# Gate and up projections begun over two of three tiles, the last tile's sums moved ahead of weight splits, and a second mixer's closing steps in another order

## The chip, the cores and the metric

The kernel runs on one core of a Trainium2 chip. A core has five engines with an instruction stream each: TensorE (PE, matrix products and transposes), VectorE (DVE), ScalarE (ACT), GpSimd (POOL) and SyncE (SP, which here only issues transfers). Each works through its stream in the order in which the build wrote it and waits on semaphores for the others. The metric is the time of one execution on the device in microseconds, the median over runs.

## The reference

A trunk of two layers over two groups of requests, 256 and 512 tokens of width 1024, all in fp32. Each layer is a token mixer (layer 0 windowed attention, layer 1 differential attention) and a SwiGLU channel mixer, both between RMS norms:

```python
def swiglu(h, w_gate_up, w_down):
    g, u = jnp.split(h @ w_gate_up, 2, axis=-1)
    return (jax.nn.silu(g) * u) @ w_down

def trunk(x, ...):
    for i in range(DEPTH):
        h = rms_norm(x, norm_mix_pre[i])
        ...
        x = x + rms_norm(m, norm_mix_post[i])
        h = rms_norm(x, norm_ffn_pre[i])
        x = x + rms_norm(swiglu(h, ffn_w_gate_up[i], ffn_w_down[i]), norm_ffn_post[i])
    return x
```

The hidden width D_FF is 2816. The mixer of layer 1 computes, for 8 heads, `(softmax(Q1 K1) - lambda softmax(Q2 K2)) V`, norms each head's result and multiplies by `w_o`.

## The kernel before

**Tiles and formats.** The 768 tokens are six tiles of 128. Activations that feed a product are kept transposed, three tiles side by side (384 columns, `HALF`): `h_hi[0]`, `h_lo[0]` hold tiles 0 to 2, `h_hi[1]`, `h_lo[1]` tiles 3 to 5. Each fp32 operand is split in two: `hi` is the rounded value (cast on ACT, L250 for weights, L331 for activations), `lo` the rest (a subtraction on DVE, L251 and L332). A product of two operands is three matmuls, hi·hi (L343), and the two mixed ones (L344, L345).

**Weights.** SP loads a raw block of 128x1024 (L224, tile `wraw` or `y_wraw`), ACT and DVE split it into `whi` and `wlo`. In gate and up the plain `wraw` tiles share two buffers; a load waits until the old block has been read for the last time. Split weights live in a ring of five units, and `free` starts the next split when a unit has been used. From the second pair on, units of gate and up come in twos from two raw blocks: four subtractions on DVE (L286 to L289) make combinations of the four quarter blocks, and the quarter called `b` is split as well.

**Gate and up (`ffn`).** They are computed by a scheme of the Strassen kind, which takes seven products for a two by two block product. The left operands are quarters of the activations and sums of them: a11, a12 (tiles 0 to 2, lower and upper half of the width), a22, s3, s1, s2, s4 (tiles 3 to 5). `combine` makes them, tile by tile in the order 0, 3, 1, 2, 4, 5: the transposes (L461), copies (L470, L475), sums (L477, L478, L479, L483) and splits (L331, L332). For each chunk c of the weights' columns the products accumulate in four banks of PSUM: X (`px`: p1 over a11, then p2 over a12), Y (`py`: p6 over s2, then p7 over s3), W (`pw`: p5 over s1, then p3 over s4) and Z (`pz`: p4 over a22). After p1 ACT copies X to `sv` (L1051), after p6 it copies Y to `u` (L1061), and only then may p7 add to the same bank; p2 ends with Silu (L1056). In chunk 0 and 1 p1 comes first, then p2 for both, then the same for chunks 2 and 3, and after that p4, p6, p5, p7 and p3 chunk by chunk. Each of these products is 12 matmuls (four slices of the contraction, three matmuls each).

**Around it.** The FFN begins while the mixer's last output tiles are still being finished: `later` holds the stages `c4, b5, d4, c5, d5` of the last two tiles (norm, scale, and as `d` the `combine`). A scheduler at build time orders each engine's instructions by their place in the program and by priority; parts under `tc.high_priority` go first, and `tc.issue_after` keeps one instruction behind another.

**End of the second mixer.** The steps of the last two heads are written out by hand in `run`: `S(h, t)` scores (`bsc`, L895), `T(h, t)` transposes of the weights of attention (`tpa`, L937), `V(h, t)` values (`pob`, L950, then L954, L956 on ACT and a scale on POOL, L963), `O(t, part)` transposes of the output heads (`tp_o`, L921). Between them stand pieces of the output product, `out[t]`: 24 matmuls of 512 columns in eight steps and an end, for the first half of the columns of tiles 0 to 2; `project` does the other tiles and the second half.

## Time and profile before

| | us |
|---|---|
| median of 3 runs | 1655.72 |
| the runs | 5599.19, 1655.11, 1655.72 |
| the profiled execution | 1656.38 |
| its span, first to last instruction | 1654.4 |
| PE busy | 1618.3 |
| DVE, ACT, POOL busy | 1222.8, 934.4, 170.7 |

The mean granted clock of PE in the profiled execution was 0.997. Layer 0's mixer ends and its gate and up products begin at about 291 us of the span, those of layer 1 at about 1157 us; the second mixer's closing steps lie around 1060 to 1107 us. The rows of the profile give a start in us, a duration in us, the engine, the line of the program, the operation, `out<-in` by the program's names, shapes, and in square brackets how long the engine had been idle and what released it. A time row of PE is longer than the distance to the next one, since matmuls are pipelined; what one costs is the distance of two starts.

### The profile page before, as it was taken

The numbers are of one execution on the slowest core, as the hardware profiler recorded it, in microseconds if no ns is written. First come the engines' busy times: TensorE is split into PE (matmuls) and PEld (weight loads), VectorE is DVE, ScalarE is ACT, GpSimd is POOL, SyncE is SP. The second block draws the span as 40 slices with busy tenths as digits, with TensorE's granted clock in tenths as the row PEclk, the third lists the DMA queues.
The fourth block names the chain that finished last, engine by engine and source line by source line (L and its number), as shares of the span: only waits on it lengthen the run. The fifth ranks groups of instructions, "written<-read, shape, count | busy, mean of one in ns | idle before, by whom it ended". The sixth has DMA issues, their size and how long they took to land. (4 is left out here: it accounts for less than half of the span.)

```text
span 1654.4 us, 24784 instructions
## 1 busy us (share of the span) xinstructions
PE 1618.3 (98%) x9163; PEld 1499.3 (91%) x9163; DVE 1222.8 (74%) x2167; ACT 934.4 (56%) x2038; POOL 170.7 (10%) x275
## 2 busy tenths in 40 slices
PE   7999999899999999999999999999899999999997
PEld 7888878899999998888999999888899999998886
DVE  7787756896766666888685886847896776656985
ACT  6777765654444444556475676766554444444553
POOL 1000001000000000001340461421000000000010
PEclk9999999999999999999999999999999999999999
DMA  6111104544333337675542332504443332337664
GB/s 217 40 39 49 37 16 153 178 137 139 101 131 110 131 116 246 239 253 180 156 111 69 98 84 79 152 1 166 153 156 123 117 125 97 131 129 254 228 238 159
DMA packets 70233, 220.64 MB, mean 133 GB/s; under 512 B 9249, under 2 KB 15521, under 8 KB 69857
## 3 DMA queue, kind: packets, MB, share of 16 engines
q1 hardware_dynamic: 54576, 175.93, 31.5%
q0 software_dynamic: 15392, 42.87, 9.1%
q8 instruction: 72, 1.18, 0.3%
q14 instruction: 49, 0.39, 0.1%
q10 hardware_dynamic: 144, 0.26, 0.0%
HBM read 163.59 MB, written 42.86 MB: 125 GB/s over the span
## 5 line engine op out<-in xcount | busy, mean ns | idle before, releaser
L251 DVE TENSOR_TENSOR wlo<-wraw,whi 128x1024 fp32r<-128x1024 f32 (+2 forms) x174 | 203.1, 1172 | 184.1 <-ACT whi L250 183.2
L250 ACT CAST whi<-wraw 128x1024 fp32r<-128x1024 f32 (+2 forms) x174 | 175.9, 1013 | 124.3 <-PE py L344 59.3
L343 PE MATMUL py<-hhi,whi 128*128 128x384 f32 x464 | 155.2, 335 | 0.3 <-ACT u L1061 0.3
L345 PE MATMUL py<-hhi,wlo 128*128 128x384 f32 x464 | 155.0, 334 | 0.0
L344 PE MATMUL py<-hlo,whi 128*128 128x384 f32 x464 | 155.0, 334 | 0.0
L331 ACT CAST hhi<-araw 128x768 fp32r<-128x768 f32 (+1 forms) x74 | 57.6, 782 | 91.3 <-DMA araw<-act 84.7
L343 PE MATMUL pv<-whi,hhi 128*128 128x512 f32 (+1 forms) x240 | 92.3, 385 | 0.0
L345 PE MATMUL pv<-whi,hlo 128*128 128x512 f32 (+1 forms) x240 | 92.2, 384 | 0.0
L344 PE MATMUL pv<-wlo,hhi 128*128 128x512 f32 (+1 forms) x240 | 92.1, 384 | 0.0
L332 DVE TENSOR_TENSOR hlo<-araw,hhi 128x768 fp32r<-128x768 f32 (+1 forms) x74 | 65.3, 889 | 32.6 <-ACT hhi L331 32.2
L343 PEld LDWEIGHTS py<-hhi,whi 128*128 128x128 f32 x464 | 87.1, 188 | 0.8 <-ACT u L1061 0.6
L344 PEld LDWEIGHTS py<-hlo,whi 128*128 128x128 f32 x464 | 87.1, 188 | 0.0
L345 PEld LDWEIGHTS py<-hhi,wlo 128*128 128x128 f32 x464 | 87.1, 188 | 0.0
L1114 POOL DMA_DIRECT2D act<-st x22 | 19.4, 882 | 636.6 <-DVE st L1113 636.6
L343 PE MATMUL po<-whi,hhi 128*128 128x512 f32 x192 | 78.4, 408 | 0.6 <-ACT hhi L331 0.6
L388 POOL TENSOR_TENSOR rstd_post<-rstd_post,mhalf 128x1 f32<-128x1 f32 x23 | 20.3, 885 | 544.9 <-ACT rstd_post L387 544.9
L345 PE MATMUL po<-whi,hlo 128*128 128x512 f32 x192 | 75.4, 393 | 0.9 <-DVE hlo L332 0.9
L901 ACT ACTIVATE be<-bsc,bmx 128x512 f32<-128x512 f32 (+1 forms) x96 | 58.7, 615 | 30.6 <-DVE bmx L899 30.0
L344 PE MATMUL po<-wlo,hhi 128*128 128x512 f32 x192 | 75.2, 392 | 0.0
L343 PE MATMUL px<-hhi,whi 128*128 128x384 f32 x208 | 69.8, 337 | 3.8 <-ACT hhi L331 2.8
L344 PE MATMUL px<-hlo,whi 128*128 128x384 f32 x208 | 69.7, 335 | 2.1 <-DVE hlo L332 2.1
L343 PE MATMUL pqa<-whi,hhi 128*128 128x384 f32 x192 | 71.1, 370 | 0.0
(307 smaller groups left out, 5049.0 us busy)
## 6 DMA issues: line engine op xcount, KB each, us to landing
act<-st POOLq DMA_DIRECT2D x22, 1344.0 KB, 6.6
wraw<-in_wgu SPq DMA_DIRECT2D x56, 512.0 KB, 4.7
araw<-act SPq DMA_DIRECT2D x70, 384.0 KB, 4.0
y_wraw<-in_wgu SPq DMA_DIRECT2D x40, 512.0 KB, 3.6
wraw<-in_wd SPq DMA_DIRECT2D x40, 512.0 KB, 4.0
xd<-x SPq DMA_DIRECT2D x18, 512.0 KB, 3.0
x<-xd SPq DMA_DIRECT2D x18, 512.0 KB, 4.3
wraw<-in_wo SPq DMA_DIRECT2D x16, 512.0 KB, 3.5
```

The costliest lines, as they stand in the source:

```text
L250: state["raw_hi"] = nc.scalar.copy(out=hi, in_=src)
L251: state["raw_lo"] = nc.vector.tensor_tensor(out=lo, in0=src, in1=hi.bitcast(F32), op=ALU.subtract)
L331: state["hi"] = nc.scalar.copy(out=hi, in_=src)
L332: state["lo"] = nc.vector.tensor_tensor(out=lo, in0=src, in1=hi.bitcast(F32), op=ALU.subtract)
L343: nc.tensor.matmul(out, ah, bh, start=start and i == 0, stop=False, skip_group_check=more)
L344: nc.tensor.matmul(out, ah, bl, start=False, stop=False, skip_group_check=more)
L345: nc.tensor.matmul(out, al, bh, start=False, stop=stop and i == last, skip_group_check=more)
L388: nc.gpsimd.tensor_tensor(out=r[:, :w], in0=r[:, :w], in1=mhalf[:, :w], op=ALU.pow)
L901: nc.scalar.activation(out=e[:, :n * P], in_=s, func=AF.Exp, bias=mx, accum_out=den[:, c:c + 1])
L1114: nc.gpsimd.dma_start(out=at_hand[c // 4][:, :, c // 2 % 2], in_=out.pop(c // 2))
```

## The change

Three things are changed. First, in `ffn` the first products of a layer (p1 of chunks 0 and 1; p4, p6 and p5 of chunk 0) are done by `early`: over the first two tiles' 256 columns for all the products of the group, and then over the third tile's 128 columns, kept behind. `mul` then skips them. All of p4(0), p6(0) and p5(0) so come before p7(0). Second, `combine` of tile 5 runs at high priority. Third, the hand-written list at the end of the second mixer weaves the output pieces of four tiles instead of three, in other places.

```diff
--- before.py
+++ after.py
@@ -340,7 +340,9 @@
 
         def step(i):
             (ah, al), (bh, bl) = pairs[i]
-            nc.tensor.matmul(out, ah, bh, start=start and i == 0, stop=False, skip_group_check=more)
+            m = nc.tensor.matmul(out, ah, bh, start=start and i == 0, stop=False, skip_group_check=more)
+            if i == 0:
+                state["first"] = m
             nc.tensor.matmul(out, ah, bl, start=False, stop=False, skip_group_check=more)
             nc.tensor.matmul(out, al, bh, start=False, stop=stop and i == last, skip_group_check=more)
 
@@ -509,7 +511,8 @@
 
         def stage_d():
             if comb is not None:
-                combine(y, t, f"h{sub + 1}_{t}", comb, o)
+                with tc.high_priority() if t == NT - 1 else ExitStack():
+                    combine(y, t, f"h{sub + 1}_{t}", comb, o)
                 return
             for s in transposes(y, t, f"h{sub + 1}_{t}"):
                 s()
@@ -1003,23 +1006,24 @@
             wk_o = column_blocks(take(4), 512)
 
             sq = {}
-            out = [out_unit(t, wk_o, o, 0, gp, sq, f"po1_0_{t}") for t in range(3)]
+            out = [out_unit(t, wk_o, o, 0, gp, sq, f"po1_0_{t}") for t in range(4)]
             S = lambda h, t: do(score, h * NT + t)
             T = lambda h, t: do(turn_e, h * NT + t)
             V = lambda h, t: do(values, h * NT + t)
             O = lambda t, part: turn_o[t][part:part + 1]
-            run = S(6, 3) + T(6, 1) + V(6, 0) + out[0][:2] + [lambda: turned(late)] + S(6, 4) + T(6, 2) + V(6, 1) + out[0][2:4]
-            run += S(6, 5) + T(6, 3) + V(6, 2) + out[1][:2] + S(7, 0) + T(6, 4) + V(6, 3) + O(0, 1) + out[1][2:4]
-            run += S(7, 1) + T(6, 5) + V(6, 4) + out[2][:2] + O(1, 1) + O(3, 0)
-            run += S(7, 2) + T(7, 0) + V(6, 5) + out[0][4:7] + O(2, 1)
-            run += S(7, 3) + T(7, 1) + V(7, 0) + out[1][4:7] + O(4, 0)
-            run += S(7, 4) + T(7, 2) + V(7, 1) + out[2][2:4] + O(0, 2) + O(5, 0)
-            run += S(7, 5) + T(7, 3) + V(7, 2) + out[0][7:] + O(1, 2) + O(3, 1)
-            run += T(7, 4) + V(7, 3) + out[2][4:7] + out[1][7:] + O(2, 2) + O(4, 1) + T(7, 5) + V(7, 4)
-            run += O(5, 1) + out[2][7:] + V(7, 5) + O(3, 2)
+            run = S(6, 3) + T(6, 1) + V(6, 0) + out[0][:3] + [lambda: turned(late)] + S(6, 4) + T(6, 2) + V(6, 1)
+            run += out[0][3:4] + out[1][:2] + S(6, 5) + T(6, 3) + V(6, 2) + out[1][2:4] + out[2][:1]
+            run += S(7, 0) + T(6, 4) + V(6, 3) + O(0, 1) + out[2][1:4]
+            run += S(7, 1) + T(6, 5) + V(6, 4) + O(3, 0) + O(1, 1) + out[0][4:7]
+            run += S(7, 2) + T(7, 0) + V(6, 5) + O(2, 1) + out[1][4:7]
+            run += S(7, 3) + T(7, 1) + V(7, 0) + O(4, 0) + out[2][4:7]
+            run += S(7, 4) + T(7, 2) + V(7, 1) + O(5, 0) + O(0, 2) + out[3][:3]
+            run += S(7, 5) + T(7, 3) + V(7, 2) + O(3, 1) + O(1, 2) + out[0][7:] + out[3][3:4]
+            run += T(7, 4) + V(7, 3) + O(4, 1) + O(2, 2) + out[1][7:] + out[3][4:7] + T(7, 5) + V(7, 4)
+            run += out[2][7:] + O(5, 1) + O(3, 2) + V(7, 5) + O(4, 2) + out[3][7:]
             for s in run:
                 s()
-        return project(o, 1, 2, lambda t: turn_o[t][2:], gp, g_next, wk_o, sq, 3)
+        return project(o, 1, 2, lambda t: turn_o[t][2:], gp, g_next, wk_o, sq, 4)
 
 
     def ffn(layer, later, comb, cpool, cstack, ostack, gains):
@@ -1030,11 +1034,29 @@
             "a11": (h_hi[0][:, 0:4], h_lo[0][:, 0:4]), "a12": (h_hi[0][:, 4:8], h_lo[0][:, 4:8]),
             "a22": (h_hi[1][:, 4:8], h_lo[1][:, 4:8]), "s3": (h_hi[1][:, 0:4], h_lo[1][:, 0:4]), **comb}
         steps = ExitStack()
+        begun, opened = set(), {}
+        two, third = slice(0, 2 * P), slice(2 * P, HALF)
         X, Y, Z, W, sv, ga, u2, u3, out = ({} for _ in range(9))
 
 
 
+        def early(banks, c, name, a, unit, part, cols):
+            if cols.start == 0:
+                banks[c] = bank(f"{name}{layer}_{c}")[:, :HALF]
+            ah, al = a_ops[a]
+            pairs = [
+                (tuple(v[:, part * 512 + k * P:part * 512 + (k + 1) * P] for v in unit), (ah[:, k, cols], al[:, k, cols]))
+                for k in range(4)]
+            if cols.start == 0:
+                products(banks[c][:, cols], pairs, True, True, True)
+                opened[c, name] = state["first"]
+            else:
+                with tc.issue_after(opened.pop((c, name)).ins):
+                    products(banks[c][:, cols], pairs, False, True, True)
+
         def mul(banks, c, name, a, unit, part, more=False):
+            if (c, name) in begun:
+                return
             if not more:
                 banks[c] = bank(f"{name}{layer}_{c}")[:, :HALF]
             ah, al = a_ops[a]
@@ -1157,7 +1179,12 @@
         c4, b5, d4, c5, d5 = later
         c4(), b5()
         u = take(2)
+        for cols in (two, third):
+            for c in range(2):
+                early(X, c, "px", "a11", u[c], 0, cols)
+        begun.update((c, "px") for c in range(2))
         p1(0, u[0]), p1(1, u[1])
+        begun.clear()
         d4()
         p2(0, u[0]), free(1), p2(1, u[1]), free(0)
         c5()
@@ -1176,9 +1203,16 @@
             return take(1)[0]
 
         u1, (u2_,) = take_u1(0), take(1)
+        for cols in (two, third):
+            early(Z, 0, "pz", "a22", u2_, 1, cols)
+            early(Y, 0, "py", "s2", u1, 1, cols)
+            early(W, 0, "pw", "s1", u2_, 0, cols)
+        begun.update(((0, "pz"), (0, "py"), (0, "pw")))
         p4(0, u2_)
         for c in range(AHEAD):
-            p6(c, u1), p5(c, u2_), p7(c, u1), c22(c), c21(c), free(0)
+            p6(c, u1), p5(c, u2_)
+            begun.clear()
+            p7(c, u1), c22(c), c21(c), free(0)
             if c + 1 < AHEAD:
                 u1, (u2_,) = take_u1(c + 1), take(1)
                 p4(c + 1, u2_)
```

The order of the instructions, before and after, at three places, the third of them on two engines. Names carry their numbers: `whi28` is weight unit 28, `wraw31` raw block 31, `py0_1` bank Y of layer 0, chunk 1, `oa5` a sum of tile 5.

PE at the start of layer 0's gate and up, around the first products of chunks 0 and 1. Before:

```order
L343 MATMUL px0_0_3749<-hhi0_110,whi24_3386 128x384
L343 MATMUL px0_1_3764<-hhi0_110,whi25_3658 128x384
L461 MATMUL tp_h1_4_1_3779<-ident_81,y_po0_1_4_3627 128x128 x4
L461 MATMUL tp_h1_4_0_3784<-ident_81,y_po0_1_4_3627 128x128 x4
L343 MATMUL px0_2_3852<-hhi0_110,whi26_3670 128x384
L344 MATMUL px0_0_3749<-hlo0_112,whi24_3386 128x384
```

After:

```order
L346 MATMUL px0_1_3762<-hlo0_112,whi25_3658 128x256
L347 MATMUL px0_1_3762<-hhi0_110,wlo25_3659 128x256
L343 MATMUL px0_0_3749<-hhi0_110,whi24_3386 128x128
L343 MATMUL px0_1_3762<-hhi0_110,whi25_3658 128x128
L463 MATMUL tp_h1_4_1_3803<-ident_81,y_po0_1_4_3627 128x128 x4
L346 MATMUL px0_0_3749<-hlo0_112,whi24_3386 128x128
```

Before, two products of 384 columns stand ahead of tile 4's transposes and of the first product with `hlo0`; after, 24 products of 256 columns do (the last two are the first rows here), and the transposes stand between products of 128 columns.

DVE between the `lo` splits of weight units 28 and 29. Before:

```order
L251 TENSOR_TENSOR wlo28_3703<-wraw29_3694,whi28_3702 128x1024
L332 TENSOR_TENSOR s1lo_0_3332<-oa4_233,s1hi_0_3331 128x4x128
L483 TENSOR_TENSOR oa1_230<-oa1_230,y_po0_1_4_3627 128x512
L251 TENSOR_TENSOR wlo29_3819<-wraw28_3674,whi29_3818 128x1024
L332 TENSOR_TENSOR s4lo_0_3336<-oa1_230,s4hi_0_3335 128x4x128
L332 TENSOR_TENSOR hlo1_113<-tp_h1_5_1_3882,hhi1_111 128x4x128
L477 TENSOR_TENSOR oa5_234<-tp_h1_5_0_3887,oa5_234 128x512
```

After (`wlo28` stands two rows above the first one, with tile 4's `s2lo` between):

```order
L332 TENSOR_TENSOR hlo1_113<-y_po0_1_4_3627,hhi1_111 128x4x128
L332 TENSOR_TENSOR s1lo_0_3332<-oa4_233,s1hi_0_3331 128x4x128
L479 TENSOR_TENSOR oa5_234<-tp_h1_5_0_3911,oa5_234 128x512
L332 TENSOR_TENSOR hlo1_113<-tp_h1_5_1_3906,hhi1_111 128x4x128
L480 TENSOR_TENSOR y_po0_1_5_3713<-tp_h1_5_0_3911,oa2_231 128x512
L481 TENSOR_TENSOR y_po0_1_5_3713<-oa5_234,oa2_231 128x512
L332 TENSOR_TENSOR s1lo_0_3332<-oa5_234,s1hi_0_3331 128x4x128
L332 TENSOR_TENSOR hlo1_113<-y_po0_1_5_3713,hhi1_111 128x4x128
L332 TENSOR_TENSOR s2lo_0_3334<-y_po0_1_5_3713,s2hi_0_3333 128x4x128
L485 TENSOR_TENSOR oa2_231<-oa2_231,y_po0_1_5_3713 128x512
L485 TENSOR_TENSOR oa1_230<-oa1_230,y_po0_1_4_3627 128x512
L251 TENSOR_TENSOR wlo29_3843<-wraw28_3674,whi29_3842 128x1024
```

Tile 5's sums and splits, which stood behind `wlo29`, now stand ahead of it, as does tile 4's `hlo`; `wlo29`, the last reader of `wraw28`, has 12 rows between it and `wlo28` where it had two.

PE at the first product of p7(0), `py0_0<-hhi1,whi28`. Before:

```order
L345 MATMUL py0_0_3975<-s2hi_0_3333,wlo28_3703 128x384
L345 MATMUL pw0_0_3991<-s1hi_0_3331,wlo29_3819 128x384
L343 MATMUL pz0_1_4044<-hhi1_111,whi31_3921 128x384
L344 MATMUL pz0_1_4044<-hlo1_113,whi31_3921 128x384
L343 MATMUL py0_1_4071<-s2hi_0_3333,whi30_3840 128x384
L344 MATMUL py0_1_4071<-s2lo_0_3334,whi30_3840 128x384
L345 MATMUL py0_1_4071<-s2hi_0_3333,wlo30_3841 128x384
L343 MATMUL py0_1_4071<-s2hi_0_3333,whi30_3840 128x384
L343 MATMUL py0_0_3975<-hhi1_111,whi28_3702 128x384
L344 MATMUL py0_0_3975<-hlo1_113,whi28_3702 128x384
```

After:

```order
L347 MATMUL pw0_0_4012<-s1hi_0_3331,wlo29_3843 128x128
L343 MATMUL pw0_0_4012<-s1hi_0_3331,whi29_3842 128x128
L346 MATMUL pw0_0_4012<-s1lo_0_3332,whi29_3842 128x128
L347 MATMUL pw0_0_4012<-s1hi_0_3331,wlo29_3843 128x128
L343 MATMUL py0_0_3999<-hhi1_111,whi28_3702 128x384
L346 MATMUL py0_0_3999<-hlo1_113,whi28_3702 128x384
```

Six products of chunk 1, which stood ahead of p7(0), now stand behind it, and the 128-column products of chunk 0 directly ahead of it.

ACT ahead of the copy of Y, `u20_0`, on which p7(0) waits. Before:

```order
L331 CAST s2hi_0_3333<-y_po0_1_5_3713 128x4x128
L250 CAST b2230_3842<-wraw31_3824 128x512
L250 CAST whi30_3840<-wraw31_3824 128x1024
L331 CAST s4hi_0_3335<-oa2_231 128x4x128
L250 CAST whi31_3921<-wraw30_3822 128x1024
L1061 COPY u20_0_3988<-py0_0_3975 128x384
```

After:

```order
L331 CAST s4hi_0_3335<-oa2_231 128x4x128
L1078 ACTIVATE ga0_3_3973<-px0_3_3891 128x384
L331 CAST s4hi_0_3335<-oa1_230 128x4x128
L250 CAST b2230_3866<-wraw31_3848 128x512
L250 CAST whi30_3864<-wraw31_3848 128x1024
L250 CAST whi31_3945<-wraw30_3846 128x1024
L1083 COPY u20_0_4061<-py0_0_3999 128x384
```

The casts of `wraw31` and `wraw30` (units 30 and 31) stand ahead of the copy in both; the cast `s4hi` of tile 2's sum moved from between them to ahead of them.

## Prediction

> **What bounds the kernel now.** I read the busy line first, then the waits of TensorE (PE), then the chain that ended last, then the timeline where the change moves rows.
>
> ```profile
> PE 1618.3 (98%) x9163; PEld 1499.3 (91%) x9163; DVE 1222.8 (74%) x2167; ACT 934.4 (56%) x2038; POOL 170.7 (10%) x275
> ```
>
> PE is busy 98% of a span of 1654.4 us, so a gain can only come out of its few gaps, and a loss is any new gap. The waits view lists the gaps by what ended them (total us, times, longest):
>
> ```profile
> PE py L344 <- DVE s2lo L332: 3.1, 2, 2.2
> PE px L343 <- ACT hhi L331: 2.8, 2, 1.5
> PE tpa L937 <- DVE be L909: 2.7, 1, 2.7
> PE px L344 <- DVE hlo L332: 2.1, 2, 1.1
> ...
> PE px L343 <- ACT sv L1051: 1.0, 1, 1.0
> PE po L345 <- DVE hlo L332: 0.9, 2, 0.7
> PE pz L343 <- ACT whi L250: 0.8, 1, 0.8
> PE tp_h L461 <- DVE y_po L397: 0.6, 2, 0.3
> ```
>
> All but the `tpa` row (second mixer) and the `po` row (not touched) stand at the heads of the two FFN layers, where the change works: 3.1 + 2.8 + 2.1 + 1.0 + 0.8 + 0.6 = 10.4 us, and 2.7 in the mixer. More than 13.1 us cannot be won by removing these. That is under 2% (33 us, about what a measurement of this kernel can tell from no change).
>
> Behind the `py <- s2lo` wait stands a loop that the chain of layer 1 shows (start, us, what):
>
> ```profile
> 1176.22 1.15 DVE wlo L251
> 1177.39 5.75 DMA wraw<-in_wgu
> 1183.39 0.63 ACT b L250
> ...
> 1190.78 0.35 PE py L343 x2
> ```
>
> A gate/up weight load takes one of two raw buffers and can start only when VectorE (DVE) has read the old contents for the last time, in the split `wlo`. Here the load is issued as `wlo` ends, and everything of the next weight unit follows its landing. The position of `wlo` on DVE sets it. Layer 0 has the same loop; the rows of DVE, of SP's queue, of ScalarE (ACT) and of PE:
>
> ```profile
> 309.11 1.22 DVE L251 TENSOR_TENSOR wlo<-wraw,whi 128x1024 fp32r<-128x1024 f32 x1
> 310.25 0.68 DVE L332 TENSOR_TENSOR s1lo<-oa,s1hi 128x512 fp32r<-128x512 f32 x1
> 310.85 0.68 DVE L483 TENSOR_TENSOR oa<-oa,y_po 128x512 f32<-128x512 f32 x1
> 311.45 1.22 DVE L251 TENSOR_TENSOR wlo<-wraw,whi 128x1024 fp32r<-128x1024 f32 x1
> ...
> 317.33 0.69 DVE L286 TENSOR_TENSOR wraw<-wraw,wraw 128x512 f32<-128x512 f32 x1 [0.46 <-DMA wraw<-in_wgu]
> ```
> ```profile
> 312.69 0.33 SPq L224 DMA_DIRECT2D wraw<-in_wgu  x1
> ```
> ```profile
> 320.50 1.06 ACT L250 CAST whi<-wraw 128x1024 fp32r<-128x1024 f32 x1 [2.56 <-DVE wraw L288]
> 321.46 0.61 ACT L331 CAST s4hi<-oa 128x512 fp32r<-128x512 f32 x1
> 321.97 1.04 ACT L250 CAST whi<-wraw 128x1024 fp32r<-128x1024 f32 x1
> 322.92 0.47 ACT L1061 COPY u<-py 128x384 f32<-128x384 f32 x1
> ...
> 333.48 0.48 ACT L1061 COPY u<-py 128x384 f32<-128x384 f32 x1 [1.71 <-DVE st L1103]
> ```
> ```profile
> 324.22 0.33 PE L343 MATMUL py<-hhi,whi 128*128 128x384 f32 x1
> 324.39 0.33 PE L344 MATMUL py<-hlo,whi 128*128 128x384 f32 x1
> ...
> 334.01 0.44 PE L343 MATMUL py<-hhi,whi 128*128 128x384 f32 x1 [0.27 <-ACT u L1061]
> ```
>
> The reader is to see: `wlo` of unit 29 (311.45) ends at 312.67 and the load of `wraw31` goes out at 312.69. DVE has it at 317.33, 4.6 us later. ACT then casts units 30 and 31 (320.50, 321.97) and only behind them copies `u` out of Y's bank (322.92). That copy lets p7(0), which accumulates s3 into the same bank, start (324.22).
>
> **The change, part by part.**
>
> *Split products.* Per layer 60 matmuls of 384 columns become 60 of 256 and 60 of 128. Start to start, 384 columns take 0.17 us (the rows at 324.22 and 324.39); narrower ones:
>
> ```profile
> 1629.83 0.28 PE L343 MATMUL pv<-whi,hhi 128*128 128x256 f32 x1
> 1629.95 0.28 PE L344 MATMUL pv<-wlo,hhi 128*128 128x256 f32 x1
> ```
> ```profile
> 25.07 0.51 PE L639 MATMUL tqa<-ident_r,sp 128*128 128x128 f32 x4
> 25.07 0.34 PE L639 MATMUL tqa<-ident_r,sp 128*128 128x128 f32 x2
> ```
>
> 256 columns take 0.12 us. The same four transposes shown whole and cut after two differ by 0.17, so 0.085 for 128. No row has a product of 128 columns in this format; the transposes are the nearest. A pair costs 0.12 + 0.085 − 0.17 = 0.035 us, 120 pairs 4.2 us. Ends: nothing (128 columns as a third of 384, 0.057; less is excluded, since the columns stay the same), or as dear as 256 columns, 0.12, 8.4 us. I take 4.2, but it need not reach the end: it lies ahead of the waits below, and PE would reach them early.
>
> The Trainium skill ("TensorE: Matmul & The Clock Gate", LDWEIGHTS) gives a weight load of P columns P/1.2 ns, 107 ns for 128. Were that the floor, a pair would cost 0.057 and all 6.8 us. The row's 0.085 is under it and is used.
>
> *The first px products.* In layer 0:
>
> ```profile
> 296.28 0.44 PE L344 MATMUL px<-hlo,whi 128*128 128x384 f32 x1 [1.07 <-DVE hlo L332]
> ```
>
> PE waited for tile 2's lo half. Now 24 products over tiles 0 and 1 (24 × 0.12 = 2.9 us) run where PE had waited for ACT's `hhi` (at most 1.5 us) and for this `hlo` (1.1). But `hlo` of tile 2 keeps its place on DVE, so PE waits again, until about 296.3. It then has 22 products of 128 columns (1.9 us) and four transposes left where it had 22 of 384 (3.8 us). That lead of about 1.5 us isn't kept: the next products accumulate into the banks that ACT copies into `sv`, and ACT now does those copies behind tile 4's copy, square and cast. I set the two against each other as 0 (ends: −3, when all px and tp_h waits of a layer go, and +1.5). Either end is swallowed by the wait at p7(0), below.
>
> *The last tile's sums first.* This carries the forecast. Between the splits of units 28 and 29 DVE now has 12 instructions where the rows above show 2; two of them stood ahead of unit 28's split before. So unit 29's split comes 8 × 0.60 (the distance of the rows at 310.25 and 310.85) = 4.8 us later. I add 0.6, one cast like 321.46's, for casts of tile 5 that DVE must await: 311.45 + 5.4 = 316.85. SP issues `wraw31` at 312.69 + 5.4 = 318.1. (The new order also puts the load of `y_wraw37` ahead of it on SP; that one waits for the sum into oa2, which DVE does before this split, so it adds nothing.) It lands by 317.33 + 5.4 = 322.7. From there the old rows took 320.50 − 317.33 = 3.2 us to unit 30's cast with five DVE instructions, now four: 2.6, so 325.3. Unit 31's cast follows without `s4hi` between them, 326.3; then the copy `u` 327.25, ended 327.7; p7(0) at about 327.8.
>
> PE is not late itself: its 36 + 36 split products of Z, Y and W take 36 × (0.12 + 0.085) = 7.4 us. They begin near 316.6 (an estimate: 24 px products, 4.1 us, behind the `sv` copies of chunks 2 and 3, which ACT now does behind tile 5's copy and cast, near 312.5) and end near 324. It waits some 3.9 us for a copy whose input is ready. Before, c = 1's first six products (1.0 us) were done by then; now none. Lateness at p7(0): 327.8 − 324.2 + 1.0 = 4.6. At p7(1), where PE waited 0.27 before, the copy `u` of 333.48 came after DVE's `st`, the end of a chain that starts from the next weights. Their buffers come free with the splits of units 30 and 31, which are late by what the landing is late, less one instruction of 0.6: 5.4 − 0.6 = 4.8 and a little for queueing. I take 5.2 us for the layer, between 4.6 and 5.4 + 0.6, and nothing given back, since behind that PE runs back to back again.
>
> What would take this away is ACT doing the copy ahead of the casts. The Trainium skill ("TensorE: Matmul & The Clock Gate", Architectural detail) says ACT and DVE are strict FIFO; the trace agrees: the copy starts at 322.92, right behind the cast that started at 321.97. Passing would leave only the wait for unit 30's weights, about 1 us per layer.
>
> Layer 1: the load issued at 1177.39 needs 5.75 us, so the same shift gives 1182.8 + 5.75 = 1188.55, unit 30's cast at 1191.2, the copy at 1193.1, p7(0) at 1193.7 against 1190.78: 2.9 + 1.0 = 3.9, and at p7(1) again about the shift of the loop, 5.0.
>
> *Second mixer's end.* Seven matmuls of 512 columns more stand ahead of the `tpa` transposes that waited 2.7 us. At 0.17 × 512 / 384 = 0.23 us each (an estimate from the rows of 384), 1.6 us of that wait go. In return the last `tp_o` transpose loses cover: 24 products (5.5 us) stood between it and the one before, now three (0.7). What feeds it ends on POOL:
>
> ```profile
> 1103.91 0.40 POOL L963 TENSOR_TENSOR ob<-ob,rstd_sub 128x128 f32<-128x128 f32 x1
> 1105.36 0.55 POOL L388 TENSOR_TENSOR rstd_sub<-rstd_sub,mhalf 128x1 f32<-128x1 f32 x1 [1.05 <-ACT rstd_sub L387]
> 1105.98 0.40 POOL L963 TENSOR_TENSOR ob<-ob,rstd_sub 128x128 f32<-128x128 f32 x1
> ```
>
> The last two tiles' `ob` come 2.1 us apart, so 2.1 − 0.7 = 1.4 us of a new wait show. Net −0.2; ends −2.7 (the old wait gone, no new one) and +2.5 (the old one stays in part and a second `tp_o` waits as long). I take 0.
>
> **Sum.** The profiled execution took 1656.4 us (span 1654.4), 0.7 above the median 1655.7. 1656.4 + 5.2 + 5.0 + 0 = 1666.6; against the median 1665.9. I say 1666.5.
>
> **Rivals.**
>
> *R1, the other side: the waits simply go.* DVE takes the last tile's sums in time it has to spare, and the copy `u` is there when PE comes. PE comes to p7(0) 3.9 us ahead of the forecast's copy, so it decides from there: unit 29's split by 316.85 − 3.9 = 312.95 and `wraw31` in by 318.8. Then 13.1 us of waits go and 4.2 come: 1656.4 − 13.1 + 4.2 = 1647.5. For it: DVE is 74% busy. Against: those ten rows follow each other without a gap, and the load is issued 0.02 us behind the split. Chance 0.11. By the price of a load in the Trainium skill, above, R1 would end at 1650.
>
> *R2, the loss grows.* The weight loop stays full in chunks 2 and 3, each adding a wait of about 1 us per layer as at `pz <- whi` (0.8): 1656.4 + 10.2 + 4 = 1670.6. For it: two raw buffers only. Chance 0.12.
>
> *R3, milder.* The load needs less than 4.6 us since it meets fewer others, or DVE is ahead by the 1 to 2 us it idles; about 2.5 us less per layer: 1661.5. Chance 0.15.
>
> **How the numbers follow.** Forecast 0.62 for 1663 to 1669, R1 0.11, R2 0.12, R3 0.15. The range 1657 to 1672 takes in R2, R3 and the mixer's ends and leaves out R1 and the far tails. No case reaches 33 us: faster 0.01, same 0.97, slower 0.02.
>
> **What the profile after would show.** A wait of `py` L343 (the first s3 product) for ACT's `u` of 3 to 5 us in each layer; `wlo` of unit 29 4 to 6 us after where it was against unit 28's; the `s2lo` and `whi` waits gone; `px <- hlo` still there; the 128-column products near 0.085 us apart. No wait at the `u` copies would make the forecast wrong and R1 right.

## The result and the profile after

| | median us | runs | profiled execution, its span |
|---|---|---|---|
| before | 1655.82 | 6 | 1656.38, 1654.4 |
| changed | 1669.74 | 6 | 1671.42, 1669.7 |

The ratio of changed to before is 1.0072, with a 95% interval of 1.0061 to 1.0083: slower by 0.72% of 1656 us, 12 us (the medians differ by 13.9). Two runs of the kernel before, one of 5599 us here and one of 2689 us beside the last experiment, are far off and enter no ratio. A second set of the changed kernel, below, gave 1.0079 (1.0065 to 1.0092). The forecast was 1666.5, in a range of 1657 to 1672.

Where the time went is read from the starts of the same instruction in both traces. The last addition to x of layer 0's mixer (L500, now L502) starts at 296.14 before and 298.07 after: 1.9 us late, in code that wasn't changed. The last gating product of layer 0's gate and up (L1103, now L1125) starts 7.3 us late, that is 5.4 more. The last addition to x of the second mixer is 8.4 late, 1.1 more. The last gating product of layer 1 is 15.3 late, 6.9 more, and so is the end of the span. The change costs 5.4 + 6.9 us in the two FFNs; the 1.9 and most of the 1.1 are scatter, which other executions below show as −0.3 to 1.7 and −1.6 to 3.1.

The busy line of the changed kernel's page, and its waits of PE (us in total, times, longest; without the 8.4 us at the kernel's entry):

```profile
PE 1631.4 (98%) x9283; PEld 1512.7 (91%) x9283; DVE 1224.8 (73%) x2167; ACT 934.5 (56%) x2038; POOL 169.3 (10%) x275
```
```profile
PE py L343 <- ACT u L1083: 5.9, 2, 3.0
PE px L343 <- ACT sv L1073: 3.9, 4, 2.3
PE px L346 <- DVE hlo L332: 2.5, 2, 1.4
PE tp_o L924 <- POOL ob L966: 2.3, 2, 1.5
...
PE tpa L940 <- ACT ob L957: 0.8, 1, 0.8
```

The wait of p7(0) for the copy `u` is new, 5.9 us in two pieces, one in each layer. The waits for `s2lo`, for `hhi` and for `whi` at `pz` are gone, those for `sv` and `hlo` are longer, and the mixer has exchanged 2.7 us of `tpa` for 1.0 more of `tp_o` and a `tpa` wait of 0.8. PE is busy 13 us longer although its share is the same: that is the 120 dearer pairs and, as will be seen, stretches at half clock.

The chain that ended last, in layer 1 (start, us, what):

```profile
1182.84 0.99 DVE wlo L251
1183.89 0.68 DVE s2lo L332
...
1189.98 1.20 DVE ob L485 x2
1191.19 1.15 DVE wlo L251
1192.35 4.85 DMA wraw<-in_wgu
1197.38 0.63 ACT b L250
...
1201.04 1.04 ACT whi L250
1202.08 0.38 ACT u L1083
1202.51 0.69 PE py L343
```

The chain now runs on DVE itself from one `wlo` (1182.84) through tile 5's sums and splits without a gap to the next `wlo` (1191.19), then through the load, the combinations, the cast and the copy `u` to PE. Before, the two `wlo` were 2.3 us apart (1173.81 and 1176.15 in the old trace). In layer 0 it is the same; rows of DVE, SP, ACT and PE:

```profile
309.08 1.22 DVE L251 TENSOR_TENSOR wlo<-wraw,whi 128x1024 fp32r<-128x1024 f32 x1
...
317.43 1.22 DVE L251 TENSOR_TENSOR wlo<-wraw,whi 128x1024 fp32r<-128x1024 f32 x1
```
```profile
318.67 11.40 SPq L224 DMA_DIRECT2D wraw<-in_wgu  x3
```
```profile
326.28 1.99 ACT L250 CAST whi<-wraw 128x1024 fp32r<-128x1024 f32 x2 [2.08 <-DVE wraw L288]
328.18 0.47 ACT L1083 COPY u<-py 128x384 f32<-128x384 f32 x1
```
```profile
328.70 0.69 PE L343 MATMUL py<-hhi,whi 128*128 128x384 f32 x1 [2.90 <-ACT u L1083]
```

`wlo` of unit 29 starts 317.43 − 309.08 = 8.4 us behind that of unit 28, where it was 2.3. The load of `wraw31`, the first of the three in SP's row, goes out behind it at 318.67; the casts of units 30 and 31 follow at 326.28, the copy `u` at 328.18, and p7(0) has waited 2.9 us.

What the prediction hadn't looked at stands in a table by stretches: us, then PE, its weight loads, DVE, ACT and POOL busy, and behind POOL's, ahead of the DMA share, the granted clock, the share of its full clock that TensorE was given. The changed kernel, from p7(0) of each layer on:

```profile
328.70:335.00 6.30, 6.30 (x20) 6.30 (x21) 4.34 (x7) 0.81 (x2) 0.00 (x0) 0.51 0.52 166
335.00:341.00 6.00, 6.00 (x37) 6.00 (x36) 4.09 (x9) 1.83 (x4) 0.00 (x0) 1.00 0.01 3
...
1202.50:1208.70 6.20, 6.19 (x19) 6.19 (x20) 4.10 (x7) 0.82 (x2) 0.00 (x0) 0.50 0.54 169
```

And the kernel before, behind its wait of 2.2 us for `s2lo` in layer 1:

```profile
1186.00:1189.90 3.90, 3.90 (x13) 3.90 (x14) 3.90 (x6) 2.88 (x4) 0.00 (x0) 0.56 0.41 126
```

Behind the wait PE runs at half clock for some 6 us: the matmuls of p7(0) start 0.32 us apart and not 0.173. In each layer 18 of them do, 2.6 us more. From 335 on the clock is full again, as the second row shows. In the FFNs of the kernel before it happened once (0.50 from 1186.5 to 1189.9), to 12 matmuls, 1.7 us. The changed kernel has one more such stretch, from 300.7 to 304.1 in layer 0; PE waits 0.2 us and 2.9 us behind it, so it is not read as a loss here.

### The profile page after: what moved, and what is told of

Same layout as the page of the kernel before. It is cut to its first block, busy times and chain, and to the rows that moved or that the text cites. A ratio compares the mean times of both kernels' runs of the same rounds, so it can differ in the third digit from the quotient of the medians.

```text
span 1669.7 us, 25027 instructions
## 1 busy us (share of the span) xinstructions
PE 1631.4 (98%) x9283; PEld 1512.7 (91%) x9283; DVE 1224.8 (73%) x2167; ACT 934.5 (56%) x2038; POOL 169.3 (10%) x275
## 5 line engine op out<-in xcount | busy, mean ns | idle before, releaser
L343 PE MATMUL px<-hhi,whi 128*128 128x384 f32 (+2 forms) x224 | 73.7, 330 | 3.9 <-ACT sv L1073 3.9
L346 PE MATMUL px<-hlo,whi 128*128 128x384 f32 (+2 forms) x224 | 73.6, 329 | 2.5 <-DVE hlo L332 2.5
L347 PE MATMUL px<-hhi,wlo 128*128 128x384 f32 (+2 forms) x224 | 73.3, 328 | 0.0
```

The source lines that it names most:

```text
L343: m = nc.tensor.matmul(out, ah, bh, start=start and i == 0, stop=False, skip_group_check=more)
L346: nc.tensor.matmul(out, ah, bl, start=False, stop=False, skip_group_check=more)
L347: nc.tensor.matmul(out, al, bh, start=False, stop=stop and i == last, skip_group_check=more)
```

## The experiments

For each run the loss in a layer is read as above: how late the last gating product of gate and up is, less how late the last addition to x of the mixer ahead of it is, both against the trace of before.

| run | median us | ratio to before, 95% interval | layer 0 | layer 1 |
|---|---|---|---|---|
| changed | 1669.74 | 1.0072 (1.0061 to 1.0083) | +5.4 | +6.9 |
| changed, again | 1671.44 | 1.0079 (1.0065 to 1.0092) | +4.2 | +7.3 |
| without the priority | 1661.50 | 1.0026 (1.0015 to 1.0037) | +1.9 | +2.0 |
| priority alone | 1655.40 | 0.9991 (0.9982 to 0.9999) | +0.5 | −2.1 |
| mixer's end alone | 1656.60 | 0.9999 (0.9991 to 1.0008) | −0.8 | −0.1 |
| changed, copy first | 1663.62 | 1.0046 (1.0032 to 1.0060) | +3.3 | +3.2 |
| changed, unit 29's split early | 1661.99 | 1.0032 (1.0020 to 1.0044) | +1.7 | +1.8 |
| Z, Y, W split alone | 1663.08 | 1.0034 (1.0021 to 1.0047) | +3.0 | +2.9 |
| X split alone | 1657.18 | 1.0003 (0.9995 to 1.0012) | +0.4 | 0.0 |
| before, copy first | 1651.44 | 0.9969 (0.9956 to 0.9981) | −4.3 | −2.0 |
| changed, both repairs | 1662.43 | 1.0032 (1.0020 to 1.0043) | +1.7 | +1.8 |
| changed, PE kept busy | 1671.07 | 1.0093 (1.0075 to 1.0111) | +5.8 | +9.0 |

The before's median beside these runs was 1656.2 to 1657.1.

**Without the priority.** The second part undone.

```diff
-                with tc.high_priority() if t == NT - 1 else ExitStack():
+                with ExitStack():
                     combine(y, t, f"h{sub + 1}_{t}", comb, o)
```

> The changed kernel with its second part undone: tile 5's sums at ordinary priority. The split wlo of unit 29 then stands 4 rows behind that of unit 28 on VectorE instead of 12 behind, 8 x 0.60 = 4.8 us earlier; the split products stay. Theory (late split, late load of raw block 31, ScalarE's casts of units 30 and 31, and the copy u behind them in order): p7(0)'s wait for u, 3.0 us in each layer, shrinks to under 1 us; what is left is TensorE's dearer products, 60 pairs x 0.058 us (0.120 + 0.111 - 0.173, from the changed kernel's rows) = 3.5 us a layer less the waits that they cover. 1659 to 1663. Rival 1 (the loss is the split products' own time on TensorE and their order ahead of p7): nothing comes back, 1668 to 1671. Rival 2 (the priority alone is the loss): 1654 to 1657.

Measured: 1661.5, as the theory has it. The new wait for `u` falls from 5.9 us in all to 2.5, and smaller ones come, `sv` 1.7 and `wlo` at `pz` 1.6 among them (its first rows behind the entry's: us in total, times, longest):

```profile
PE px L346 <- DVE hlo L332: 2.7, 2, 1.4
PE py L343 <- ACT u L1083: 2.5, 3, 1.7
```

At p7(0) only 0.2 of the 2.5 us are left, in layer 1. The others, 0.6 us in layer 0 and 1.7 in layer 1, are at p7(1), the same product of chunk 1. Two thirds of the loss come with the priority. The rest is there without it.

**The priority alone.** Only that line added to the kernel before.

```diff
-                combine(y, t, f"h{sub + 1}_{t}", comb, o)
+                with tc.high_priority() if t == NT - 1 else ExitStack():
+                    combine(y, t, f"h{sub + 1}_{t}", comb, o)
```

> The kernel before with the second part alone: tile 5's sums at high priority, no split products, the mixer as before. On VectorE the split of unit 29 is as late as in the changed kernel (11 rows between it and that of unit 28), but on ScalarE the copy u of bank Y now stands ahead of the casts of units 30 and 31. Theory (the late load hurts because the copy u stands behind the late casts): p7(0) doesn't wait for u; TensorE waits only for unit 30's weights after p7(0), about as long as it waited for them and for s2lo before: 1655 to 1659. Rival (a split that is late by 5 us costs 5 us a layer wherever the copy stands): 1664 to 1667.

Measured: 1655.4, no loss at all. This is the sharpest of the runs, since the split is as late as in the changed kernel. DVE's two `wlo` are 7.8 us apart, and unit 30 is cast at 326.19; but ACT's copy `u` (318.40) stands far ahead of the casts:

```profile
309.55 1.22 DVE L251 TENSOR_TENSOR wlo<-wraw,whi 128x1024 fp32r<-128x1024 f32 x1
...
317.30 1.22 DVE L251 TENSOR_TENSOR wlo<-wraw,whi 128x1024 fp32r<-128x1024 f32 x1
```
```profile
318.40 0.48 ACT L1062 COPY u<-py 128x384 f32<-128x384 f32 x1 [0.96 <-PE py L345]
...
326.19 2.11 ACT L250 CAST whi<-wraw 128x1024 fp32r<-128x1024 f32 x2 [1.26 <-DVE wraw L288]
```
```profile
328.36 0.44 PE L343 MATMUL pz<-hhi,whi 128*128 128x384 f32 x1 [1.86 <-ACT whi L250]
```

p7(0) runs while the load is under way, and PE waits only 1.9 us in layer 0, for the weights of chunk 1. That is no loss on balance, since the `s2lo` waits (3.1 us in the two layers) are gone too; waits for `whi` of 3.6 us, where there were 0.8, stand in their place. A late split alone doesn't cost 5 us; a late split with `u` behind its casts, and nothing else for PE to do, does. So 13.9 us isn't the sum of the parts: the priority alone gives −1.4, the rest without the priority +4.7, and together they lose 12 to 14.

**The mixer's end alone.** The third part on the kernel before.

```diff
-            out = [out_unit(t, wk_o, o, 0, gp, sq, f"po1_0_{t}") for t in range(3)]
+            out = [out_unit(t, wk_o, o, 0, gp, sq, f"po1_0_{t}") for t in range(4)]
...
-            run += O(5, 1) + out[2][7:] + V(7, 5) + O(3, 2)
+            run += out[2][7:] + O(5, 1) + O(3, 2) + V(7, 5) + O(4, 2) + out[3][7:]
...
-        return project(o, 1, 2, lambda t: turn_o[t][2:], gp, g_next, wk_o, sq, 3)
+        return project(o, 1, 2, lambda t: turn_o[t][2:], gp, g_next, wk_o, sq, 4)
```

> The kernel before with the third part alone, the other order of steps at the second mixer's end. Forecast: 0 (ends -2.7 and +2.5): the tpa wait of 2.7 us shrinks to about 1 and a tp_o wait of 1.4 us comes. 1655 to 1657. Rival (the new tp_o waits, 1.5 and 0.7 us in the changed kernel, outweigh it): 1658 to 1659.

Measured: 1656.6, the same within 0.1%. The old `tpa` wait for `be` of 2.7 us is gone from its waits (two of 0.4 and 0.3 us are there instead), and `tp_o` waits 2.3 us in two pieces where it waited 1.3 in one.

**The copy first.** The changed kernel, with the splits of weight unit 30 and later issued behind the first copy `u`.

```diff
             kind, r, n = units[i]
+            if i >= state.get("cap", len(units)):
+                fetch(r[1] + 1)
+                return
...
-            nc.scalar.copy(out=u2[c], in_=Y[c])
+            state["u2"] = nc.scalar.copy(out=u2[c], in_=Y[c])
...
+        state["cap"] = state["used"] + 6
         c4(), b5()
...
-            p6(c, u1), p5(c, u2_)
+            p6(c, u1)
+            if c == 0:
+                state.pop("cap")
+                with tc.issue_after(state["u2"].ins):
+                    free(2)
+            p5(c, u2_)
```

> The changed kernel in full, except that the splits of weight unit 30 and those after it are issued only after the copy u of chunk 0's bank Y, so ScalarE copies u ahead of the casts. The late load stays. Theory: the wait for u at p7(0) (3.0 us in each layer) goes, and TensorE waits next for unit 30's and 31's weights, which are as late as before: 1.5 to 2 us of the 5.4 to 6.9 us per layer come back: 1664 to 1667. Rival 1 (the place of the copy is the whole cause): 1657 to 1661. Rival 2 (the copy's place is nothing, the weights set the end anyway): 1669 to 1671.

Measured: 1663.6, 0.4 below what the theory gave. The waits for `u` are gone from the view; `pz` waits 2.2 us for `whi` in both layers together. In the prediction the passing of the casts would have left about 1 us a layer; 3.2 stayed. The split products' own time on PE, 3.5 us a layer (60 pairs at 0.058), is of that size; that it is what stays is not shown by this run alone.

**Unit 29's split early.** The other repair: the changed kernel, and one cast and one `wlo` at high priority too.

```diff
+        state["early"] = state["used"] + 5
         c4(), b5()
...
+                if i == state.get("early"):
+                    after.enter_context(tc.high_priority())
                 two_parts(hi[:, :n], lo[:, :n], src[:, :n])
```

> The changed kernel in full, but the split of weight unit 29 (one cast, one wlo) is at high priority too. On VectorE wlo of unit 29 then stands one row behind that of unit 28 instead of 12; tile 5's sums stay ahead of everything else, and u stays behind the casts. Theory (the late wlo is what the priority costs): raw block 31 is loaded 6 to 7 us earlier, p7(0)'s wait for u of 3.0 us falls under 1 us in each layer, and the loss falls to that of the kernel without the priority: 1660 to 1663. Rival (the sums ahead of the other weight work cost in themselves, or units 30 and 31 do): 1667 to 1671.

Measured: 1662.0, inside the theory's range. With tile 5's sums still first, only unit 29's `wlo` moved, to 1.7 us behind that of unit 28:

```profile
308.97 1.23 DVE L251 TENSOR_TENSOR wlo<-wraw,whi 128x1024 fp32r<-128x1024 f32 x1
...
310.71 1.22 DVE L251 TENSOR_TENSOR wlo<-wraw,whi 128x1024 fp32r<-128x1024 f32 x1
```

p7(0) doesn't wait any more in either layer (at p7(1) there are waits for `u` of 0.6 and 1.3 us), and 3.7 and 5.1 us of the two layers' loss are gone. The place of one unit's split carries what the priority cost.

**Z, Y and W alone, X alone.** Of the first part only the products of chunk 0 ahead of p7(0), and only those of X; mixer and priority as before.

```diff
+        for cols in (two, third):
+            early(Z, 0, "pz", "a22", u2_, 1, cols)
+            early(Y, 0, "py", "s2", u1, 1, cols)
+            early(W, 0, "pw", "s1", u2_, 0, cols)
+        begun.update(((0, "pz"), (0, "py"), (0, "pw")))
```

> The kernel before with only p4, p6 and p5 of chunk 0 done in two passes (256 and 128 columns), all ahead of p7(0). Theory: with the load on time, what stays is TensorE's own time, 36 pairs x 0.058 = 2.1 us a layer, and a wait for u at p7(0) under 1 us, since chunk 1's six products no longer stand ahead of it; the s2lo waits (3.1 us in both layers) go, as the 128-column pass needs tile 5 later: 1657 to 1661. Rival (this part alone is the whole loss of the change): 1666 or more.

```diff
+        for cols in (two, third):
+            for c in range(2):
+                early(X, c, "px", "a11", u[c], 0, cols)
+        begun.update((c, "px") for c in range(2))
```

> The kernel before with only the first products of X (chunks 0 and 1) done in two passes. Theory: 24 pairs x 0.058 = 1.4 us a layer more on TensorE against the hhi waits of 1.4 us a layer that go; hlo's wait stays: 1655 to 1658. Rival (the waits go with nothing behind them): 1650 to 1653.

Measured: 1663.1 and 1657.2. X in two passes is free: 48 pairs at 0.058 are 2.8 us, and the `hhi` waits that go were 2.8. Z, Y and W in two passes lose 3 us a layer, 2 us over the theory's upper end: 36 pairs × 0.058 are 2.1. The rest shows at another place in each layer. In layer 0 the load of `wraw31` took 7.0 us (4.5 in the kernel before), PE waited 1.8 us for `s2lo`, and the clock was 0.50 for 6.8 us behind that. In layer 1 the load was on time and p7(0) started 2.1 us earlier against the layer's start than in the kernel before; of the wait for `u` of 3.2 us only 0.7 is at p7(0), and 2.5 are at p7(1):

```profile
1193.45 0.44 PE L343 MATMUL py<-hhi,whi 128*128 128x384 f32 x1 [0.74 <-ACT u L1082]
...
1206.64 0.44 PE L343 MATMUL py<-hhi,whi 128*128 128x384 f32 x1 [2.49 <-ACT u L1082]
```

So the part of the loss that comes without the priority arises for the most part between p7(0) and p7(1), as in the run without the priority. The split of Z, Y and W and the order (six products of chunk 1 now behind p7(0)) were changed together in every run, so which of them brings that wait is not shown.

**The kernel before, copy first.** The edit of the copy-first run on the kernel before.

> The kernel before, with the splits of weight unit 30 and those after it issued only after the copy u of chunk 0's bank Y, as in the run with the copy first: ScalarE copies u ahead of the casts, and on VectorE tile 5's last sums stand ahead of unit 30's combinations, without any of the three parts of the change. Theory (p7(0) waits on what stands ahead of u in ScalarE's order): the waits of py for s2lo (3.1 us), of pz for whi (0.8) shrink and p7(0) runs while the load is under way: 3 to 6 us faster than before, 1650 to 1653. Rival (the loop of load and split sets the pace in chunk 1 anyway): 1655 to 1657.

Measured: 1651.4, ratio 0.9969, faster than both kernels. ACT copies `u` at 319.56, ahead of the casts of units 30 and 31, and the waits of PE at `py`, at `pz` and for `sv` are all gone (the first rows of its waits, without the entry's):

```profile
319.56 0.48 ACT L1064 COPY u<-py 128x384 f32<-128x384 f32 x1 [1.04 <-PE py L348]
319.93 0.62 ACT L250 CAST b<-wraw 128x512 fp32r<-128x512 f32 x1
...
322.04 2.00 ACT L250 CAST whi<-wraw 128x1024 fp32r<-128x1024 f32 x2
```
```profile
PE px L346 <- ACT hhi L334: 2.8, 2, 1.4
PE tpa L940 <- DVE be L912: 2.6, 1, 2.6
```

In the kernel before, `u` started at 322.92, right behind the cast of 321.97; here it starts 3.4 us earlier, 4.6 with the 1.2 us by which this execution is late already. So the kernel before had the queueing of `u` behind the casts too, in a milder form. How much of the 5 us is the copy's own is not shown: the edit also puts tile 5's last sums ahead of unit 30's combinations on DVE (its `s2lo` starts at 316.58, where it stood between the combinations at 319.18), and the `s2lo` waits, 3.1 us, go with that.

**Both repairs.** The changed kernel with the copy first and unit 29's split early (the two diffs above together).

> The changed kernel with both repairs of the earlier runs: unit 29's split at high priority, and the splits of unit 30 and later behind the copy u of chunk 0. Theory: neither the late load nor the copy's place holds p7(0) any more, the waits of py for u are gone, and what is left of the change is TensorE's dearer products: 120 pairs x 0.058 = 7.0 us, less the hhi and s2lo waits they cover (2.8 + 3.1) but with hlo's and sv's kept: 1657 to 1662, not below the kernel with the split early alone by more than 3. Rival (the two repairs each take a different 3 us a layer and add up): 1654 to 1656, about the kernel before.

Measured: 1662.4, 0.4 over the theory's range and far from the rival: the repairs don't add up. Each removes the same wait, since p7(0) needs either weights that are early or a copy that doesn't queue behind them. The early split is enough by itself (1.7 and 1.8 us a layer, with or without the copy first); the copy first alone leaves 3.3 and 3.2, so with the copy ahead the late split still costs 1.5 us a layer. What is left is PE's: 7.0 us of dearer pairs, for waits that took other forms (for `sv` 4.1, `hlo` 2.3, `whi` 2.2, `st` 1.1, 9.7 together, against 10.4 before). Less the 1.7 us of half clock, of which this execution has none in the FFNs, that makes 4.6; the medians give 5.4, the two layers of the trace 3.5.

**The change again.**

> The changed kernel as it is, once more, on the chip and beside the runs of the kernel before that the run with both repairs uses. It tells the size of the loss and of its two layers' shares from another execution: 1667 to 1671, ratio 1.006 to 1.009; the loss in layer 1 (6.9 us in the first profile, 5.4 in layer 0) falls to 5 to 6 if the longer load there (5.4 us against 4.3) was chance, and stays near 7 if the new order makes it.

Measured: 1671.4. The loss in layer 1 stays near 7 us (7.3). The first load took 4.3 us where the other execution had 5.4, and unit 29's `wlo` is 5.4 us late and not 6.5; but the load of `wraw31` behind it, issued at 1190.24, took 6.6 us where it had 4.85, so that PE waits 4.8 us at p7(0) and not 3.0. The lengths of the loads were chance, and the loss hangs on both; here they nearly cancel. In layer 0 the loss is 1.2 us smaller, and the table by stretches shows why: behind nearly the same wait (2.9 us) the clock is low for half as long as the 6.8 us from 328.0 to 334.9 in the other execution.

```profile
327.30:330.70 3.40, 3.34 (x10) 3.34 (x11) 1.54 (x2) 0.39 (x2) 0.00 (x0) 0.50 0.61 186
330.70:334.20 3.50, 3.50 (x21) 3.50 (x21) 3.31 (x6) 0.48 (x1) 0.00 (x0) 1.00 0.32 119
```

Nine matmuls and not 18 start 0.32 us apart, 1.3 us less, and PE doesn't wait at p7(1).

**PE kept busy.** The changed kernel, and 25 matmuls of 128 columns in each layer between the last first product and p7(0); they write to columns of a bank that nothing reads, and the output doesn't use them. `state["mm"]` is the last matmul of a product, `state["pz"]` the whole bank Z.

```diff
+        for k in range(25):
+            with tc.issue_after(state["mm"].ins):
+                state["mm"] = nc.tensor.matmul(
+                    state["pz"][:, HALF:], u2_[0][:, :P], h_hi[1][:, 0, :P], start=True, stop=True, skip_group_check=True)
```

> The changed kernel in full, with 25 more matmuls of 128 columns per layer (25 x 0.111 = 2.8 us) between the last first product and p7(0), into the 128 columns of Z's bank that nothing uses: TensorE works through the wait for u (3.0 us) in place of idling. Nothing is computed with them. Theory (new, from the changed kernel's trace: after the wait the granted clock is 0.51 for 6.3 us in layer 0 and 0.50 for 6.2 us in layer 1, and matmuls of 384 columns start 0.32 us apart instead of 0.173, 2.6 us more per layer): the clock stays at 1.0 behind the wait, p7(0) starts when it did, and 3 to 5 us come back though work was added: 1665 to 1668. Rival (the low clock has another cause, such as the load or the cast running then, or what it costs is waited for afterwards anyway): 1669.5 to 1672, and the clock behind p7(0)'s start again near 0.5.

Measured: 1671.1, the rival's time. The clock did stay up; its granted value behind p7(0)'s start is 1.00 (the row of the table by stretches, for layer 0; in layer 1 it is the same), so idling was what lowered it. But PE, without the 2.6 us of half clock, waits 1.8 us for `u` at p7(1) and 0.8 for `wlo`:

```profile
327.00:331.00 4.00, 4.00 (x27) 3.91 (x27) 2.66 (x3) 1.92 (x4) 0.00 (x0) 1.00 0.43 142
```
```profile
325.27 2.95 PE L1214 MATMUL pz<-hhi,whi 128*128 128x128 f32 x25
328.18 0.44 PE L343 MATMUL py<-hhi,whi 128*128 128x384 f32 x1
...
340.70 0.44 PE L343 MATMUL py<-hhi,whi 128*128 128x384 f32 x1 [1.83 <-ACT u L1084]
...
344.22 0.44 PE L347 MATMUL pz<-hhi,wlo 128*128 128x384 f32 x1 [0.81 <-DVE wlo L251]
```

So here the loop of load, split and copy sets the end of chunk 1. That the half clock of the changed kernel only fills time that would be waited for does not follow, since the filler changed DVE's order as well. DVE now waits for the next load (5.0 us, 4.1 in the changed kernel) ahead of its sum of `u` and `sv`:

```profile
334.26 0.69 DVE L286 TENSOR_TENSOR wraw<-y_wraw,wraw 128x512 f32<-128x512 f32 x1 [1.17 <-DMA wraw<-in_wgu]
334.99 0.69 DVE L287 TENSOR_TENSOR y_wraw<-y_wraw 128x512 f32<-128x512 f32 x1
335.60 0.55 DVE L1091 TENSOR_TENSOR u<-u,sv 128x384 f32<-128x384 f32 x1
```

In the changed kernel the sum stood ahead:

```profile
333.46 0.56 DVE L1090 TENSOR_TENSOR u<-u,sv 128x384 f32<-128x384 f32 x1
333.94 0.69 DVE L286 TENSOR_TENSOR wraw<-y_wraw,wraw 128x512 f32<-128x512 f32 x1
```

And with the order unchanged, in the second execution of the changed kernel, half as much half clock went with 1.2 us less loss. In layer 1 the loss was 9.0 in this execution; a wait for `sv` of 2.6 us and a half-clock stretch from 1172.5 to 1179.3, both ahead of the filler, are part of it.

## Why the prediction came out as it did

**What bounds the kernel** was right: 13 us of waits to win, and a new gap to lose. Its 33 us for what a measurement can tell was far too coarse: the intervals above are 3 to 6 us wide. R1 needed unit 29's split by 312.95 on the old clock of the trace; it came at 317.43 − 1.9 = 315.5.

**The last tile's sums.** The mechanism was right, and the runs show each link: one `wlo` moved (early split) or the copy moved (copy first) takes the wait at p7(0) away. The size of the shift was put at 5.4 us for both layers. Taking off what each layer was late already, `wlo` of unit 29 was 4.1 us late in layer 0 (DVE didn't have to await the casts for which 0.6 was added, and caught up a little) and 6.5 in layer 1, there with a longer load ahead of unit 28's split (4.1 and 5.4 in the second execution). p7(0) started 328.70 − 1.9 = 326.8, against 327.8 predicted. That PE came to p7(0) near 324, as predicted, is luck: its split products began at 317.1 − 1.9 = 315.2 and not 316.6, and were dearer by about as much.

**p7(1)** was the step with the wrong event. The prediction had the loss grow there, by 0.6 us in layer 0 and 1.1 in layer 1, behind the copy `u` of chunk 1; PE doesn't wait there in either execution of the changed kernel. In its place p7(0) and what follows ran at half clock, 2.6 us a layer, a term that the prediction doesn't have. For layer 0 the account is then: p7(0) later by 2.6, six products not done ahead of it 1.0, half clock 2.6, waits behind it that the old kernel had and the new one hasn't 0.7: 2.6 + 1.0 + 2.6 − 0.7 = 5.5, measured 5.4 (predicted 5.2). For layer 1: 3.3 + 1.0 + 2.6 = 6.9, measured 6.9 (predicted 5.0, short by 1.9).

The second execution bears the account out: 2.6 + 1.0 + 1.3 − 0.7 = 4.2 in layer 0, measured 4.2, and 3.9 + 1.0 + 2.6 = 7.5 in layer 1, measured 7.3. So the mechanism up to p7(0) was right, and that the sum came near is in part luck: 5.2 us of half clock were left out, and against them stood a growth of 1.7 us that didn't come and, in layer 0, 1.0 us too much lateness at p7(0). The chain that the text puts ahead of p7(1) is there all the same: where p7(0) isn't held up, PE waits for `u` at p7(1), 0.6 and 1.7 us without the priority, 0.6 and 1.3 with the split early.

**Split products.** Taken at 0.085 us for 128 columns from four transposes, they start 0.111 us apart:

```profile
321.84 0.27 PE L347 MATMUL pz<-hhi,wlo 128*128 128x128 f32 x1
321.95 0.27 PE L343 MATMUL pz<-hhi,whi 128*128 128x128 f32 x1
```

A pair costs 0.12 + 0.111 − 0.173 = 0.058, and all 7.0 us, inside the ends given (up to 8.4) but not the 4.2 chosen: transposes were the wrong neighbour. The price of a weight load in the Trainium skill ("TensorE: Matmul & The Clock Gate", LDWEIGHTS), 107 ns for 128 columns, was set aside there, and the trace agrees with it to 4%. That it is hidden behind the wait at p7(0) fits the account of the full change above, which needs no term for it; without the priority, or with a repair, losses of 1.7 to 3.3 us a layer stay that are of its size.

**The first px products** came to 0, as said: PE still waits for `hlo` (2.5 us in both layers), the `sv` copies behind tile 4's work cost 3.9 us in all, and X in two passes alone gives 1.0003. **The second mixer's end** came to 0 (0.9999).

**The rivals.** R1 fell. R2's waits in chunks 2 and 3 aren't in the view of waits, and R3's shorter load wasn't seen (4.8 and 4.85 us). That ACT does the copy behind casts whose input comes late is one half of the cause, the late split the other: with either put right the wait at p7(0) is gone, and with the copy ahead a split just as late costs nothing on balance (priority alone). In the changed kernel the early split takes back all that the priority cost, the copy first only part of it.

What stays open: what part of the half clock would come back if the clock stayed up and DVE's order didn't change; what brings the wait at p7(1) when Z, Y and W alone are split; and the scatter of 1 to 3 us in stages that weren't changed. Several of these contain stretches at half clock, but no run tells these apart from the length of loads.

## What to carry to other kernels

Before raising the priority of one group of work, look at what it is put ahead of on that engine, and whether that is the last reader of a buffer that a load waits for: a few sums moved ahead of one split cost 8 to 10 us together with the split products, and nothing without them. A copy that frees an accumulator shouldn't stand in a queue behind casts of weights that are still to arrive; holding that weight work behind the copy took 5 us off the kernel before, where the change added 12. Splitting matmuls into narrow pieces to start early cost 0.058 us for each matmul split here, so it is worth it only where a wait of the same size is really covered.

## What the hardware showed

A wait of PE of 2 to 3 us can be dearer than its length: behind p7(0)'s wait the granted clock was 0.50 to 0.51 for 6.2 to 6.3 us. The Trainium skill ("TensorE: Matmul & The Clock Gate", What's actually happening) gives half clock after an idle window of about 3.4 us. Here shorter waits were enough, and 2.95 us of filler matmuls kept the clock at 1.00. It is not the length alone that counts. In the kernel before the clock was 0.50 for 3.4 us behind the wait of 2.2 us for `s2lo` (1186.5 to 1189.9), and for 3.4 us from 1067.0 on, behind the wait of 2.7 us for `tpa`. In layer 0 of the second execution it was 0.50 for 3.4 us behind 2.9 us. In the run with the copy first a wait of 2.3 us for `sv` (until 311.95) left it at 1.00. The depth was half clock each time; what decides whether it drops, and whether for 3.4 or 6.8 us, no run here tells.
